# Where the tiles of the second FFN product lie, and in which order its weights are loaded

## The chip, the cores and the metric

The kernel runs on one core of a Trainium2 chip. The metric is the device time of one execution in microseconds (us). The core has TensorE (PE, matmuls), VectorE (DVE), ScalarE (ACT), GpSimd (POOL) and SyncE (SP), whose queue issues the loads from HBM. All five work through instruction streams of their own, in order, and wait on each other by semaphores. SBUF gives each of the 128 partitions some 207 KB to the program's tiles here, which it lays out itself.

## The reference

One step of a decoder layer over 1088 tokens (1024 of a prompt, 8 x 8 of samples) with 1024 channels:

```
x = x + 0.5 * swiglu(rmsnorm(x), w_ffn1_in, w_ffn1_out)
x = x + mixer(rmsnorm(x)) @ w_out        # gated DeltaNet and attention, gated
x = x + 0.5 * swiglu(rmsnorm(x), w_ffn2_in, w_ffn2_out)
y = rmsnorm(x)

swiglu(x, w_in, w_out): gate, up = split(x @ w_in); (silu(gate) * up) @ w_out
```

The hidden width of both FFNs is 2816, 22 blocks of 128. All is float32.

## The kernel before

Each float32 product is made of three matmuls: an operand z is split into hi (ACT casts it, L225) and lo = z - hi (DVE subtracts, L226), and hi·hi, hi·lo and lo·hi are summed in PSUM. So an operand is ready when its load has landed, ACT has cast and DVE has subtracted.

An FFN is two products. `ffn_in` computes the hidden values h from x, in seven Strassen products per pair of 128-blocks, into a gate buffer `sg` (pool of two buffers). `store_h` writes the results to DRAM, `hq` (seven combinations, for 18 blocks) or `hd` (the last four blocks); GpSimd issues these stores. The operands are x7[0] and x7[1], the seven combinations of the two token halves p = 0 (256 columns a matmul) and p = 1 (288). The last pair of blocks runs all seven products of p = 0 first and then all seven of p = 1 (L497), so that x7[0] is done with earlier than x7[1].

`ffn_out` multiplies h by w_out, Strassen again: seven passes j over five groups of blocks (`GROUPS`; four of two block pairs, one of one), and four direct blocks at the end. `rights` loads the h tiles (544 KB) from hq into h0 and h1 in turn and splits them into x0 to x3. `lefts` loads w_out into w0 to w3 and v, one tile per group, in two halves: load(i, 0) brings the rows of a11 and a21 of group i, load(i, 1) those of a12 and a22 (1024 KB each, 512 for group 4). It splits the pass's combination into u0 to u3. GpSimd changes the w tiles in place for later passes (L634, L636), and in pass 2 DVE makes the difference S = a22 - a11 (L629). Nothing of ffn_out can start before x0, u0 of group 0 stand; its matmuls are L689 (hi·hi), L690 (hi·lo of h) and L691.

The order of the instructions on each queue is not that of the code: a scheduler sets it when the program is built, from its own estimate of when places and operands come free; `keep_in_program_order` pins single instructions (the first two splits of each side). What an instruction truly waits for at run time is the last user of the bytes that it writes, and what it reads.

`open_ffn_out` puts the tiles of a second product into one pool growing from the bottom and one ("right") ending at the top, in the order named. The sizes per partition in bytes are acc 34816, tq 26112, w 16384, x 8704, u and v and f 8192, h and r 4352, S 4096. The places are those of the first product's tiles, so a load waits for the last of these. By the sizes the places are, before and after, and what stands there in the last stretch of the first product:

| tile | FFN1 before | FFN1 after | FFN2 before | FFN2 after |
|---|---|---|---|---|
| w0 | sg buffer | x7[0] | x7[1] | x7[0] hi |
| h0, h1 | x7[0] | x7[0] | x7[1] | x7[0] hi |
| w1 | sg buffer | x7[0], "tt" and "xr" | x7[0] lo | x7[0] lo |
| w2 | x7[0] | in tq: x7[1] | x7[0] hi | x7[1] |
| w3 | in tq: x7[1] | sg buffer | x7[0] hi | x7[1], x7[0] hi |
| v | in tq: x7[1] | in tq: x7[1] | "tm" | "tm" |

The last sg buffer is free when the store of hd has landed, x7[0] at the end of p = 0, x7[1] at the end of p = 1. In FFN2 x7[0] is in two parts: its hi lies on the place of an older tile, xhl[0], its lo beside x7[1]. acc lies on x7[1] before and after; x1 and x2 change places, so that x2 instead of x1 overlaps the last sg buffer, as S0 and S1 do.

`ffn_in_first` makes the first pair of blocks of FFN1; its gate tile of token half 1, sg0, takes one of two buffers "raw7" that otherwise hold raw weights (1024 KB loads, `pair_raw`, L297). `turned` transposes x in nine blocks of 128 tokens during ffn_in of FFN1: load into the tile "xr" (L544), TensorE (L551), ACT back into xr (L554), GpSimd's store (L555).

Of the kernel before, what the change touches and what calls it, by code (L numbers as in the profile page):

```python
# [9 lines left out]
F32 = mybir.dt.float32  # L10
# [8 lines left out]
P = 128  # L19
D = 1024  # L20
KD = D // P
# [19 lines left out]
GROUPS = ((0, 2), (2, 2), (4, 2), (6, 2), (8, 1))  # L41
# [69 lines left out]
class Weave:  # L111
# [28 lines left out]
    def run(self, n, *until):  # L140
        self.left += n
        while self.cur is not None or self.left or any(g in until for _, g in self.lat):
            due = [e for e in self.lat if e[0] <= self.t]
            if due:
                e = due[0]
                try:
                    cost, gap = next(e[1])
                    self.t += cost
                    e[0] = self.t + gap
                except StopIteration:  # L150
                    self.lat.remove(e)
            elif not self.fill():
                self.t = min(e[0] for e in self.lat)


class Core:
# [234 lines left out]
    def ffn_in_first(self, st, w_in):  # L391
        nc, v = self.nc, self.nc.vector
# [42 lines left out]
        def quadrants(p, col, h, ts):  # L435
            for k in range(4):
                b = self.tm("b").rearrange("p a b -> p (a b)")[:, :4 * h].rearrange("p (a b) -> p a b", a=4)
                self.xn_chunk(k, [x[t] for t in ts], 2 * h, b)
                oh, ol = (y[:, :, k, col:col + h] for y in self.x7[p])
                self.split(oh[:, 0:4], ol[:, 0:4], b)  # L440
                self.t_parts(b)
                self.split(oh[:, 4:7], ol[:, 4:7], b[:, 1:4])
# [16 lines left out]
        self.columns_t(rows)  # L459
        ug = list(self.units_direct(raws[0]))  # L460
        quadrants(1, 0, P, (4, 5))
        sg = self.rawp.tile([P, KD, 2 * P], F32, tag="raw7", bufs=2, name=self.name("sg0")).rearrange("p a b -> p (a b)")[:, :4 * 288]
        s2 = sg.rearrange("p (m h t) -> p m h t", m=2, h=2)
        direct(1, 0, P, 0, ug, s2)
        norm(*plan[1])
# [12 lines left out]
        sg = self.sg("sg0")  # L478
# [59 lines left out]
    def turned(self):  # L538

        nc = self.nc  # L540
        for t in range(NCH):
            m = min(P, T - t * P)
            xr = self.ttp.tile([P, D], F32, tag="xr", bufs=1, name=self.name("xr"))
            nc.gpsimd.dma_start(xr[:m], self.x_rows(t))  # L544
            for _ in range(4):
                yield
            pts = []
            for hf in range(2):
                pts.append(self.bank("t").rearrange("p (a b) -> p a b", b=P))
                for k in range(4):  # L550
                    nc.tensor.transpose(out=pts[hf][:, k, :m], in_=xr[:m, (4 * hf + k) * P:(4 * hf + k + 1) * P], identity=self.ident[:m, :m])  # L551
            y = xr.rearrange("p (k t) -> p k t", t=P)
            for hf in range(2):
                nc.scalar.copy(y[:, 4 * hf:4 * hf + 4, :m], pts[hf][:, :, :m])  # L554
            nc.gpsimd.dma_start(self.xt[:, :, t * P:t * P + m], y[:, :, :m])  # L555
            for _ in range(5):
                yield

    def open_ffn_out(self, layout):

        shapes = {"acc": [P, 4, 4, HT], "tq": [P, 3, 4, HT], "x": [P, 2, T], "u": [P, 2, D], "h": [P, T], "w": [P, 2, 2, D], "v": [P, 1, 2, D], "S": [P, D], "r": [P, T], "f": [P, 2, D]}
        self.fo = {}
        for stack, side, names in layout:
            pool = self.pool("fo", stack=stack, side=side)
            for nm in names.split():
                k = nm if nm in shapes else nm.rstrip("0123456789")
                self.fo[nm] = pool.tile(shapes[k], F32R if k in "xuf" else F32, name=self.name(nm))
        self.acc = self.fo["acc"]
        if "tq" in self.fo:
            flat = self.fo["tq"].rearrange("p a b c -> p (a b c)")  # L570
            self.fo["w3"] = flat[:, :4 * D].rearrange("p (n k c) -> p n k c", n=2, k=2)
            self.fo["v"] = flat[:, 4 * D:6 * D].rearrange("p (n k c) -> p n k c", n=1, k=2)

    def x(self, k, c):
# [29 lines left out]
    def lefts(self, w_out):  # L604

        fo, dma, g, v = self.fo, self.nc.sync.dma_start, self.nc.gpsimd, self.nc.vector
        ws = [fo[f"w{i}"] for i in range(4)] + [fo["v"]]

        def load(i, k):
            if i < len(GROUPS):  # L610
                p, n = GROUPS[i]
                dma(ws[i][:, :, k], w_out[0, 2 * p * P:2 * (p + n) * P, :].rearrange("(n k p) c -> k p n c", k=2, p=P)[k])

        def quads(i):
            return [ws[i][:, :, k, 512 * h:512 * h + 512] for k in range(2) for h in range(2)]

        at = 0
        for i in range(3):
            load(i, 0)
        for j in range(7):  # L620
            for i in range(len(GROUPS)):
                a11, a21, a12, a22 = quads(i)
                if j == 0:
                    load(i + 3, 0)
                    load(i, 1)
                if j == 2:
                    n = GROUPS[i][1]
                    s = fo[f"S{i % 2}"].rearrange("p (n c) -> p n c", c=512)[:, :n]
                    v.tensor_tensor(out=s, in0=a22, in1=a11, op=ALU.subtract)  # L629
                    g.tensor_tensor(out=a12, in0=a12, in1=s, op=ALU.subtract)  # L630
                out = self.split_to(f"u{at % 4}", (a11, a12, s if j == 2 else None, a11, a22, a21, a12)[j], at < 2)
                at += 1
                if j == 0:
                    g.tensor_tensor(out=a11, in0=a11, in1=a21, op=ALU.subtract)  # L634
                if j == 1:
                    g.tensor_tensor(out=a21, in0=a21, in1=a22, op=ALU.add)  # L636
                yield out
        for i, f in enumerate(DIRECT):
            if i == 0:
                for k in range(2):  # L640
                    dma(fo[f"S{k}"], w_out[0, (f + k) * P:(f + k + 1) * P, :])
            out = self.split_to(f"u{at % 4}", fo[f"S{i % 2}"].rearrange("p (n c) -> p n c", n=1))
            at += 1
            if i < 2:
                dma(fo[f"S{i}"], w_out[0, (f + 2) * P:(f + 3) * P, :])
            yield out
# [986 lines left out]
    def ffn2(self):  # L1633
        nc, v = self.nc, self.nc.vector
        self.lab = ""
        wo = self.i["w_out"].rearrange("o (k p) c -> p (o k) c", p=P)
        with ExitStack() as st:
# [4 lines left out]
            x0 = self.pool("x0", stack=s0).tile([P, KD, 512], F32, name="x0")  # L1642
            x1 = self.pool("x1", stack=s1).tile([P, KD, 576], F32, name="x1")
            ap, aq = self.pool("ain", stack=sa, side="right"), self.pool("ain", stack=sa)
            aq.tile([P, 1408], F32, name="gap")
            a = {h: (aq if h in (4, 5) else ap).tile([P, T], F32, tag="al" if h in (2, 3, 6) else "ah", bufs=2, name=self.name("a")) for h in (2, 3, 0, 1, 4, 5, 6)}
# [101 lines left out]
        order = (0, 2, 1)  # L1748
        with ExitStack() as st:
            self.open_psum(st, t=8)  # L1750
            self.open_ffn_out(((st, None, "u1 u2 u3 x3 x0 u0 S0 S1 x1 x2 v r0 w1"), (st, "right", "h0 h1 w0 acc w2 w3")))
            self.ffn_out(self.i["w_ffn2_out"], self.final(order), self.xd, order, lambda: None)

    def final(self, order):
# [98 lines left out]
    def run(self):  # L1853
        self.setup()
        with ExitStack() as st:
            self.open_psum(st, t=8)
            self.open_ffn_in(st)
            self.table(ACT_FFN)
            self.ffn_in_first(st, self.i["w_ffn1_in"])
            self.ffn_in(self.i["w_ffn1_in"], [(f, up, (0, 1)) for f in range(2, NF, 2) for up in range(2)], self.turned())  # L1860
        order = (0, 2, 1)
        with ExitStack() as st, ExitStack() as se:
            self.open_psum(st, t=8)
            self.open_ffn_out(((st, None, "acc tq x0 u0 x1 u1 x2 u2 x3 u3 S0 f"), (se, "right", "S1 w2 h0 h1 w0 w1")))

            def between():
                se.close()
                self.open_xhl()
                raw = self.fo["S0"].rearrange("p (k c) -> p k c", c=P)
                nc = self.nc  # L1870
                nc.sync.dma_start(raw, self.i["w_in"].rearrange("o (k p) c -> p (o k) c", p=P)[:, :, O_KS:O_KS + P])
                self.first_w = [self.fo["f"][:, i].rearrange("p (k c) -> p k c", c=P) for i in range(2)]
                self.split(*self.first_w, raw)

            self.ffn_out(self.i["w_ffn1_out"], self.to_mixer(order), self.xt, order, between)
        self.mixer()
        self.ffn2()
# [44 lines left out]
```

## Time and profile before

| | us |
|---|---|
| median of 3 runs | 2888.87 (2887.42 to 2890.08) |
| the profiled execution | 2897.63 |
| its span in the profile | 2895.9 |
| TensorE busy | 2703.3 (93%) |

The profile is of one execution; its span is the time from the first to the last instruction, and 1.7 us of the execution's time lie around it. Places in it are given in us from the span's start. FFN1's first product ends at about 544, its second runs from about 578 to beyond 776; FFN2's first product ends at about 2613, its second runs from 2639. A row of a timeline gives the start, the duration, engine, line, operation, the tiles out<-in and, in brackets, how long the engine had been idle before it and what ended this. PE's clock is given as a share of 2.4 GHz; 0.50 is 1.2 GHz.

### The profile page before, as it was taken

How to read it: one execution, taken by the hardware profiler on the slowest of the kernel's cores; microseconds unless marked ns; L12 is line 12 of the kernel's file. 1: busy time of each engine (PE TensorE's matmuls, PEld its weight loads, DVE VectorE, ACT ScalarE, POOL GpSimd, SP SyncE). 2: the span in 40 equal slices, each digit the busy share in tenths (PEclk: the TensorE clock that was granted, in tenths of full speed). 3: DMA queues.
4: the chain of work that ended last, by engine and by line, in shares of the span. 5: the costliest groups of instructions: out<-in, count | busy, mean ns of one | idle time of the engine just before them, and what ended most of it. 6: DMA issues, size and time to landing. Idle time of an engine off the chain costs nothing. (4 is left out here: it accounts for less than half of the span.)

```text
span 2895.9 us, 50870 instructions
## 1 busy us (share of the span) xinstructions
PE 2703.3 (93%) x19839; PEld 2527.8 (87%) x19839; DVE 1987.4 (69%) x4497; ACT 1242.7 (43%) x2919; POOL 656.0 (23%) x625
## 2 busy tenths in 40 slices
PE   6999999599989999999999999999989999996998
PEld 6899999599978888878788888888979999996998
DVE  6677787455563767666786767775689888765545
ACT  5233323133333667663654555556444332322333
POOL 3221221131031211121223121222044122104110
PEclk9999999799999999999999999999999999998999
DMA  3233422454432322344234243324614232216462
GB/s 134 93 127 116 141 99 80 148 160 115 133 103 61 82 64 57 82 106 97 61 92 103 60 100 78 92 65 140 217 62 133 95 113 99 91 53 238 116 151 78
DMA packets 236871, 306.66 MB, mean 106 GB/s; under 512 B 14405, under 2 KB 184214, under 8 KB 236598
## 3 DMA queue, kind: packets, MB, share of 16 engines
q1 hardware_dynamic: 203252, 222.21, 25.5%
q0 software_dynamic: 33312, 81.19, 10.5%
q8 instruction: 156, 2.56, 0.4%
q14 instruction: 85, 0.70, 0.1%
q10 hardware_dynamic: 66, 0.02, 0.0%
HBM read 212.19 MB, written 84.19 MB: 102 GB/s over the span
## 5 line engine op out<-in xcount | busy, mean ns | idle before, releaser
L251 PE MATMUL pst<-x,u 128*128 128x256 f32 (+3 forms) x2640 | 779.3, 295 | 1.0 <-DVE x L226 1.0
L250 PE MATMUL pst<-x,u 128*128 128x256 f32 (+3 forms) x2024 | 609.8, 302 | 18.2 <-ACT x L225 10.5
L252 PE MATMUL pst<-x,u 128*128 128x256 f32 (+3 forms) x2024 | 606.2, 300 | 10.5 <-DVE u L226 10.5
L251 PEld LDWEIGHTS pst<-x,u 128*128 128x128 f32 x2640 | 504.2, 191 | 6.9 <-DVE x L226 1.3
L250 PEld LDWEIGHTS pst<-x,u 128*128 128x128 f32 x2024 | 387.4, 192 | 26.8 <-ACT x L225 12.1
L252 PEld LDWEIGHTS pst<-x,u 128*128 128x128 f32 x2024 | 388.6, 192 | 16.7 <-DVE u L226 12.1
L689 PE MATMUL pst<-x,u 128*128 128x272 f32 x1008 | 290.9, 290 | 50.5 <-ACT x L225 50.5
L225 ACT CAST u<-raw 128x512 fp32r<-128x512 f32 x316 | 190.6, 617 | 304.6 <-PE pst L252 268.8
L252 PE MATMUL psgh<-xhl,wlh 128*128 128x512 f32 (+2 forms) x912 | 304.1, 333 | 0.0
L690 PE MATMUL pst<-x,u 128*128 128x272 f32 x1008 | 292.9, 291 | 5.2 <-DVE x L226 5.2
L691 PE MATMUL pst<-x,u 128*128 128x272 f32 x1008 | 292.4, 290 | 0.0
L226 DVE TENSOR_TENSOR u<-raw,u 128x512 fp32r<-128x512 f32 x316 | 226.6, 725 | 42.6 <-ACT u L225 42.4
L334 DVE TENSOR_TENSOR tm<-pst,tm 128x288 f32<-128x288 f32 (+1 forms) x420 | 177.1, 436 | 104.8 <-PE pst L252 103.2
L252 PE MATMUL pst<-xhl,u 128*128 128x256 f32 (+2 forms) x808 | 235.9, 292 | 3.3 <-DVE u L226 3.3
L250 PE MATMUL pst<-xhl,u 128*128 128x256 f32 (+2 forms) x808 | 236.1, 294 | 2.7 <-ACT u L225 2.7
L689 PEld LDWEIGHTS pst<-x,u 128*128 128x128 f32 x1008 | 190.7, 190 | 51.0 <-ACT x L225 51.0
L690 PEld LDWEIGHTS pst<-x,u 128*128 128x128 f32 x1008 | 191.8, 190 | 5.9 <-DVE x L226 5.9
L691 PEld LDWEIGHTS pst<-x,u 128*128 128x128 f32 x1008 | 191.6, 190 | 0.0
L252 PEld LDWEIGHTS psgh<-xhl,wlh 128*128 128x128 f32 x912 | 173.8, 191 | 12.4
L252 PEld LDWEIGHTS pst<-xhl,u 128*128 128x128 f32 x808 | 152.6, 189 | 7.1 <-DVE u L226 4.1
L250 PEld LDWEIGHTS pst<-xhl,u 128*128 128x128 f32 x808 | 152.2, 189 | 6.0 <-ACT u L225 3.1
L250 PE MATMUL psg<-xhl,whc 128*128 128x512 f32 (+2 forms) x456 | 155.2, 340 | 1.4 <-ACT whc L225 1.4
(693 smaller groups left out, 6454.1 us busy)
## 6 DMA issues: line engine op xcount, KB each, us to landing
raw<-in_w_ffn_in_dram SPq DMA_DIRECT2D x48, 1024.0 KB
h<-hq SPq DMA_DIRECT2D x56, 544.0 KB
hq<-sg POOLq DMA_DIRECT2D x45, 544.0 KB, 3.7
rawh<-in_w_in_dram SPq DMA_DIRECT2D x38, 512.0 KB
w<-in_w_ffn_out_dram SPq DMA_DIRECT2D x14, 1024.0 KB
raw<-in_w_in_dram SPq DMA_DIRECT2D x21, 512.0 KB
ring<-ring SPq DMA_DIRECT2D x32, 272.0 KB
t4h<-tdr POOLq DMA_DIRECT2D x32, 256.0 KB, 5.6
```

The lines of the kernel that those rows point to most:

```text
L225: keep(self.nc.scalar.copy(hi, src))
L226: return keep(self.nc.vector.tensor_tensor(out=lo, in0=src, in1=hi.bitcast(F32), op=ALU.subtract))
L250: nc.tensor.matmul(out, w[0], x[0], start=start, stop=False)
L251: nc.tensor.matmul(out, w[0], x[1], start=False, stop=False)
L252: nc.tensor.matmul(out, w[1], x[0], start=False, stop=stop)
L334: v.tensor_tensor(out=out, in0=pb, in1=t[:, i, :n], op=ALU.add)
L689: nc.tensor.matmul(pb, w[0], y[0], start=first, stop=False, skip_group_check=True)
L690: nc.tensor.matmul(pb, w[0], y[1], start=False, stop=False, skip_group_check=True)
L691: nc.tensor.matmul(pb, w[1], y[0], start=False, stop=end, skip_group_check=True)
```

## The change

The memory maps of both second products, as in the table above; w2 instead of w3 shares the place of tq in FFN1. The order of `load` calls in `lefts`: before, the first halves of groups 0, 1, 2, then in pass 0 at group i load(i+3, 0) and load(i, 1); after, load(0, 0) alone, then (1, 0), (2, 0), (0, 1) at group 1, (3, 0), (1, 1) at group 2, (4, 0), (2, 1) at group 3, (3, 1) at group 4, and (4, 1) at group 0 of pass 1. And sg0 of `ffn_in_first` goes from a raw7 buffer to the tile "xr", which is widened from 1024 to 1152 columns. The pools' sizes stay as they were but for xr. No arithmetic changes.

```diff
--- before.py
+++ after.py
@@ -459,7 +459,7 @@
         self.columns_t(rows)
         ug = list(self.units_direct(raws[0]))
         quadrants(1, 0, P, (4, 5))
-        sg = self.rawp.tile([P, KD, 2 * P], F32, tag="raw7", bufs=2, name=self.name("sg0")).rearrange("p a b -> p (a b)")[:, :4 * 288]
+        sg = self.ttp.tile([P, 4 * 288], F32, tag="xr", bufs=1, name=self.name("sg0"))
         s2 = sg.rearrange("p (m h t) -> p m h t", m=2, h=2)
         direct(1, 0, P, 0, ug, s2)
         norm(*plan[1])
@@ -540,7 +540,7 @@
         nc = self.nc
         for t in range(NCH):
             m = min(P, T - t * P)
-            xr = self.ttp.tile([P, D], F32, tag="xr", bufs=1, name=self.name("xr"))
+            xr = self.ttp.tile([P, 4 * 288], F32, tag="xr", bufs=1, name=self.name("xr"))[:, :D]
             nc.gpsimd.dma_start(xr[:m], self.x_rows(t))
             for _ in range(4):
                 yield
@@ -568,7 +568,7 @@
         self.acc = self.fo["acc"]
         if "tq" in self.fo:
             flat = self.fo["tq"].rearrange("p a b c -> p (a b c)")
-            self.fo["w3"] = flat[:, :4 * D].rearrange("p (n k c) -> p n k c", n=2, k=2)
+            self.fo["w2"] = flat[:, :4 * D].rearrange("p (n k c) -> p n k c", n=2, k=2)
             self.fo["v"] = flat[:, 4 * D:6 * D].rearrange("p (n k c) -> p n k c", n=1, k=2)
 
     def x(self, k, c):
@@ -615,14 +615,17 @@
             return [ws[i][:, :, k, 512 * h:512 * h + 512] for k in range(2) for h in range(2)]
 
         at = 0
-        for i in range(3):
-            load(i, 0)
+        load(0, 0)
         for j in range(7):
             for i in range(len(GROUPS)):
                 a11, a21, a12, a22 = quads(i)
-                if j == 0:
-                    load(i + 3, 0)
-                    load(i, 1)
+                if j == 0 and i:
+                    if i == 1:
+                        load(1, 0)
+                    load(i + 1, 0)
+                    load(i - 1, 1)
+                if j == 1 and i == 0:
+                    load(len(GROUPS) - 1, 1)
                 if j == 2:
                     n = GROUPS[i][1]
                     s = fo[f"S{i % 2}"].rearrange("p (n c) -> p n c", c=512)[:, :n]
@@ -1748,7 +1751,7 @@
         order = (0, 2, 1)
         with ExitStack() as st:
             self.open_psum(st, t=8)
-            self.open_ffn_out(((st, None, "u1 u2 u3 x3 x0 u0 S0 S1 x1 x2 v r0 w1"), (st, "right", "h0 h1 w0 acc w2 w3")))
+            self.open_ffn_out(((st, None, "u1 u2 u3 x3 x0 u0 S0 S1 x2 x1 v r0 w1"), (st, "right", "acc w2 w3 h0 h1 w0")))
             self.ffn_out(self.i["w_ffn2_out"], self.final(order), self.xd, order, lambda: None)
 
     def final(self, order):
@@ -1861,7 +1864,7 @@
         order = (0, 2, 1)
         with ExitStack() as st, ExitStack() as se:
             self.open_psum(st, t=8)
-            self.open_ffn_out(((st, None, "acc tq x0 u0 x1 u1 x2 u2 x3 u3 S0 f"), (se, "right", "S1 w2 h0 h1 w0 w1")))
+            self.open_ffn_out(((st, None, "acc tq S0 x0 u0 x2 u2 x3 u3 f x1 u1"), (se, "right", "h0 h1 w0 w1 w3 S1")))
 
             def between():
                 se.close()
```

## Rows read from the trace of the kernel before

**Rows 1.** The page, part 1: busy us, share and instructions of each engine.

```profile
PE 2703.3 (93%) x19839; PEld 2527.8 (87%) x19839; DVE 1987.4 (69%) x4497; ACT 1242.7 (43%) x2919; POOL 656.0 (23%) x625
```

**Rows 2.** Windows: us, busy us (count) by engine, granted clock, DMA share, GB/s.

```profile
149.00:160.00 11.00, 5.03 (x33) 4.14 (x32) 9.74 (x8) 4.22 (x8) 8.84 (x9) 0.93 0.59 199
160.00:544.00 384.00, 384.00 (x3049) 383.77 (x3049) 291.07 (x515) 118.25 (x243) 72.80 (x70) 0.99 0.30 101
544.00:578.00 34.00, 2.52 (x13) 1.97 (x12) 11.69 (x9) 6.28 (x6) 13.37 (x6) 0.55 0.81 297
560.00:570.00 10.00, 0.00 (x0) 0.00 (x0) 1.47 (x2) 2.09 (x2) 2.34 (x1) 0.50 1.00 398
578.00:776.00 198.00, 198.00 (x1537) 196.73 (x1538) 109.55 (x128) 70.40 (x81) 40.78 (x22) 0.99 0.52 139
2613.00:2640.00 27.00, 2.77 (x13) 2.22 (x12) 11.89 (x8) 6.18 (x6) 11.04 (x5) 0.56 0.89 335
2639.00:2840.00 201.00, 200.73 (x1548) 198.97 (x1549) 113.84 (x130) 71.52 (x81) 44.60 (x23) 0.99 0.53 142
```

**Rows 3.** Timeline of PE: start, us, instruction, count, idle before and releaser.

```profile
577.90 0.60 PE L690 MATMUL pst<-x,u 128*128 128x272 f32 x1 [2.63 <-DVE x L226]
...
2602.18 0.30 PE L250 MATMUL pst<-x,u 128*128 128x288 f32 x1
...
2639.27 0.59 PE L690 MATMUL pst<-x,u 128*128 128x272 f32 x1 [2.58 <-DVE x L226]
```

**Rows 4.** Timeline of the load queue (SPq), 540 to 580.

```profile
544.82 1.35 SPq L612 DMA_DIRECT2D tq<-in_w_ffn_out_dram  x3
557.87 2.15 SPq L612 DMA_DIRECT2D w<-in_w_ffn_out_dram  x4
560.07 1.27 SPq L594 DMA_DIRECT2D h<-hq  x2
```

**Rows 5.** Waits of SP, 540 to 580: us, times, longest.

```profile
SPq L612 <- PE pst L252: 64.5, 1, 64.5
SPq L612 <- DMA hd<-sg: 11.4, 1, 11.4
```

**Rows 6.** Timeline of POOL, 541 to 582.

```profile
546.22 0.72 POOL L519 DMA_DIRECT2D hd<-sg  x1 [41.50 <-DVE sg L341]
...
557.51 2.34 POOL L636 TENSOR_TENSOR tq<-tq 128x1024 f32<-128x1024 f32 x1 [2.10 <-DMA tq<-in_w_ffn_out_dram]
```

**Rows 7.** Timeline of ACT, 544 to 582.

```profile
572.62 1.10 ACT L225 CAST x<-h 128x1088 fp32r<-128x1088 f32 x1 [2.90 <-DMA h<-hq]
```

**Rows 8.** Timeline of DVE, 541 to 582.

```profile
574.40 3.44 DVE L226 TENSOR_TENSOR x<-h,x 128x1088 fp32r<-128x1088 f32 x1
...
578.90 1.28 DVE L226 TENSOR_TENSOR x<-h,x 128x1088 fp32r<-128x1088 f32 x1
```

**Rows 9.** Chain that ended last, 2600 to 2645: start, us, what.

```profile
2613.57 0.37 SPq L612
...
2615.94 16.64 DMA w<-in_w_ffn_out_dram
2632.70 1.36 DVE S L629
...
2635.77 3.46 DVE x L226
```

**Rows 10.** Timeline of DVE, 2600 to 2642.

```profile
2614.07 0.46 DVE L341 TENSOR_TENSOR sg<-sg,tm 128x288 f32<-128x288 f32 x1
2620.34 1.23 DVE L226 TENSOR_TENSOR u<-w,u 128x1024 fp32r<-128x1024 f32 x1 [5.81 <-ACT u L225]
```

**Rows 11.** Waits of SP, 30 to 200: us, times, longest.

```profile
SPq L297 <- DMA hq<-sg: 46.7, 2, 43.5
```

**Rows 12.** Waits of ACT, 100 to 540: us, times, longest.

```profile
ACT xr L554 <- PE pst L551: 18.2, 1, 18.2
```

**Rows 13.** The page, part 6: DMA issues, KB each, us to landing.

```profile
hq<-sg POOLq DMA_DIRECT2D x45, 544.0 KB, 3.7
```

## The prediction

> **What bounds the kernel now.** I read the page first: TensorE is busy in 2703.3 of 2895.9 us, so what a change of layout can bring is in the other 193 us [rows 1]. Then windows on both sides of the two places where a first FFN product gives way to its second product. In 544 to 578 TensorE works 2.52 of 34 us, in 2613 to 2640 it works 2.77 of 27; once the second product runs it has no gap (198.00 of 198, 200.73 of 201) [rows 2]. So two holes, some 33 and 26 us up to the matmuls at 577.90 and 2639.27 from which it runs through [rows 3], hold nearly all that these edits can reach.
>
> What fills the holes is on the load queue (SP). In FFN1 it sits until TensorE's last matmul, issues three loads into the tile tq at 544.82, then sits 11.4 us for the store of hd from sg before it issues w0 at 557.87 and the first h at 560.07 [rows 4, 5]. The store was issued at 546.22 [rows 6]. h0 is behind four w tiles, so its hi cast comes at 572.62 [rows 7]; its lo follows, 3.44 us long and ending at 577.84, and TensorE's full run starts at 577.90 [rows 3, 8]. In FFN2 the chain that ended last reads: loads issued from 2613.57, 16.64 us of a w load, the subtraction S, h0's lo from 2635.77 [rows 9]. No load is issued before the last matmul of the first product, though half p = 0 is done when the 288-column matmuls begin, at 2602.18 [rows 3].
>
> **FFN1.** Before, w0 and w1 lie on the gate buffer sg, w2, h0, h1 on the place of x7[0]. After, h0, h1, w0, w1 lie on x7[0] and the old turning buffer, and w3 and S1 on sg. w0 and h0 so wait for half p = 0 alone. Does SP come to them then? In the rows before, h0's place was free when p = 0 ended, yet h was issued at 560.07 [rows 4]: the instruction order on the queue goes by whole pools of tiles, and the pool "acc tq ..." comes first. w2 and v are in tq now, so I expect three loads into tq at 544.82 again, (2,0), (4,0), (2,1), and w0 and h0 right behind them, without the 11.4 us.
>
> By bytes: those three are 2.62 MB, the store 1.11, w0 1.05, h0 0.56: 5.34 MB. At 398 GB/s, the rate of 560 to 570 [rows 2], that is 13.4 us. The lag on top comes from two rows. The third tq load came in at 557.51 [rows 6]: 12.7 us after issue, less 9.4 us for 3.73 MB, is 3.3. h0's cast at 572.62, 14.75 us after w0's issue, less 11.9 us for 4.75 MB, is 2.85 [rows 4, 7]. So h0 lands at about 544.82 + 13.4 + 3 = 561.2, its hi is done at 562.3 (cast 1.10 [rows 7]), and its lo takes 1.28 us or 3.44 [rows 8]: full run at 563.6 to 565.7. Should w1's first half be ahead of h0, 1.05 MB more, 2.6 us: 568.3. I take 566.5, the middle, a gain of 11.4, called 11. Ends: 14.3 (563.6), and 8 if both w1 and another half tile are ahead.
>
> The DMA page of the Trainium skill ("DMA: Bandwidth & Descriptors", section Specifications) gives about 358 GB/s of HBM for a core; by that 5.34 MB would take 14.9 us and the gain would be 1.5 us less. The row shows 398 in this kernel, with one core running, so the row decides.
>
> **FFN2.** Before, w0, h0, h1 lie on x7[1], which is read up to the last matmul. After, they lie on xhl[0], where p = 0's operands stood: free at 2602.18. w1 stays on the rest of p = 0's operands; acc, w2 and most of w3 lie on x7[1] now. I expect w0 and h0 first on the queue (the pool that holds them is freed as a whole by TensorE, the left one only by the store), issued at 2602.2. 1.61 MB at 398 GB/s is 4 us, with 3 us of lag 2609.3, before p = 1 ends (2613.57 [rows 9]); ACT casts the hi parts at once. DVE has the last combination until 2614.53 [rows 10], then u0's lo (1.23 us [rows 10]) to 2615.8 and h0's lo to 2617.0 or 2619.2, by 1.28 or 3.46 us [rows 8, 9]. Gain against 2639.27: 22.3 or 20.1; I take 21. Bound below: w0 and h0 are issued at 2613.57 after all, but first: with the store 2.72 MB, 6.8 + 3 us, 2623.4, hi and lo 2.4 to 4.6: 2627 at the middle, a gain of 12.
>
> The 1.28 or 3.46 us is where the Trainium skill bears ("SBUF — State Buffer", section Who interferes with whom): a VectorE tensor-tensor on two SBUF inputs and a GpSimd instruction that reads SBUF exclude each other, and the one that starts first runs through. By that rule GpSimd's subtraction (L634), released by u0's lo, loses to h0's lo if that stands ready right behind u0's lo: 1.28, a gain of 22.3, and 3.46 would need a GpSimd instruction already running. The rows have both lengths for the same shape, and I leave the middle.
>
> **What is left over.** The clock is low after either hole (0.55 and 0.56 granted, of 2.4 GHz, in the windows [rows 2]) and stays so for some microseconds, before and after alike: 0. The order of left tiles, S0 and x1 against x2, and "f" behind x3 move tiles whose first use is later than h0's: covered by j = 0, which has six groups of work; bound 2.6 us a product, one half tile at 398 GB/s, if one comes too late. The running second product draws 139 GB/s where 398 were there [rows 2], so starving it beyond that is no case of mine.
>
> **The start.** sg0 leaves a raw7 buffer for the tile "xr". A raw load waited 43.5 us for a store of hq from sg0 [rows 11]; that wait goes, but the load's data was wanted only when the next weights were cast, and from 160 to 544 TensorE has no gap (384.00 of 384 [rows 2]), so 0. In exchange the first turned block loads only when sg0's last store has landed (instead of at the start), and its first transposes come after ffn_in_first anyway. One gap hangs on a turned block already: ACT sits 18.16 us before L554 for the transposes of one block, weight casts queue behind it, and TensorE works 5.03 of 11 us in 149 to 160 [rows 2, 12]: 6 us. If the other order closes it, -6; if the load blocks GpSimd for its wait, +3.7 (a store's landing [rows 13]). I take 0.
>
> **The sum.** -11 - 21 + 0 = -32. The profiled execution took 2897.63 us (span 2895.9), so 2865.6 by its own time; it lies 8.8 above the median 2888.87 of the shown runs, for which the same 32 gives 2857. The main case's own range: FFN1 8 to 14, FFN2 12 to 22, start +4 to -6, stalls up to 5; all ends at once are unlikely, and I take 2846 to 2872.
>
> **Rivals.**
> (a) Both products get early loads: FFN1's w0 and h0 go out when p = 0 ends. In FFN2 half p = 1 takes 11.4 us (2602.18 to 2613.57), so that is near 533.4 here; they land at about 540.4, the lo parts wait only for DVE's last combination, which released the store at 546.22 [rows 6], and full run is at 548.7 to 550.9: FFN1 gains 28, the total is 49, 2840. Against it: the order by pools above [rows 4]. Chance 0.15.
> (b) The S subtraction of the third pass (L629) stays ahead of h0's lo on DVE, as it is in the chain now [rows 9], and now waits for a half tile that is loaded later. Up to (0,1) FFN1 has 7.99 MB, 20.1 us, at 567.9; S 3.2 and lo 3.44 bring 574.5: a gain of 3.4. FFN2, issued behind (2,0) from 2613.57: 3.2 MB, 8.1 + 3 us, 2624.6, S and lo to 2631.2: a gain of 8. Together 11, 2878. DVE's order is set when the program is made, and a half tile that comes later moves S back as well, which speaks against it. Chance 0.1.
> (c) The change doesn't do what it says: SP still comes to w0 and h0 at 557.87, and in FFN2 h0 stays behind the other w tiles. No gain, 2889. Chance 0.07.
> (d) Slower: the turning of x. With sg0 in the tile of xr every turned block shifts against the weight units; the row of 18.16 us shows that one badly placed block costs 6 us [rows 12]. There are nine blocks (the loop of L541). From six more such blocks on it outweighs the 32; with all nine, 8 more than now, 48 - 32 = +16: 2905. For it: ACT's casts are queued behind L554. Against: 160 to 544 runs free of gaps now [rows 2], though blocks are turned there too. Chance 0.07.
>
> **Chances.** Main case 0.61, (a) 0.15, (b) 0.1, (c) 0.07, (d) 0.07. 0.2%, 5.8 us, is about what a measurement here can tell from no change: faster 0.86, same 0.07, slower 0.07. The range goes from (a) to (b), 2838 to 2880, and leaves out (c) and (d).
>
> **What would show it.** SP's issue of w0 and h near 546 instead of 557.87 (FFN1) and near 2602 (FFN2), before the last matmul; no wait for hd ahead of w; the restart at about 566 less the start's shift, and 3.5 to 6 us after the last combination in FFN2; windows of the second products still without a gap; the gap at 149 to 160 where it was. The prediction is wrong if h0 still lands behind several w tiles, if DVE or ACT has another instruction ahead of h0's parts, if half tiles of the first pass come so late that TensorE stops between groups, or if the turning shows new gaps before 544.

## The result, and the profile after

The changed kernel takes 2847.87 us (median of 4 runs, 2846.10 to 2850.15), the kernel before 2888.14 beside it: a ratio of 0.986, with a 95% interval of 0.9843 to 0.9877, 40 us less. The forecast was 32 less, 2857, with 2838 to 2880 as the range. That the two are so near is in part luck, for behind it stand two misses that partly cancel: the start brought some 18 us that I had put at 0, and some 14 us came back in the second products, where I had allowed 2.6 us each and taken none.

The page of the changed kernel, part 1, answers to [rows 1]: TensorE's busy time hardly moves, the span around it does. The changed kernel has three lines more, so the matmuls L689 to L691 are L692 to L694 here, GpSimd's L634 and L636 are L637 and L639, and S (L629) is L632.

```profile
PE 2691.0 (95%) x19839; PEld 2516.7 (88%) x19839; DVE 1997.3 (70%) x4497; ACT 1243.1 (44%) x2919; POOL 659.1 (23%) x625
```

Windows of the changed kernel (columns as in [rows 2]). The gap at 149 to 160 is gone (5.03 of 11 before), the hole in FFN1 goes from 526 to 547.4, and the second products, which had no gap [rows 2], now have some: 193.88 of 196.6 in FFN1, and in FFN2 25.71 of the first 35.6 us behind the first product, the short hole among them.

```profile
149.00:160.00 11.00, 11.00 (x90) 11.00 (x89) 6.05 (x13) 3.04 (x7) 1.63 (x2) 1.00 0.31 100
160.00:526.00 366.00, 366.00 (x2923) 365.63 (x2921) 280.18 (x494) 113.35 (x232) 72.80 (x70) 1.00 0.30 102
526.00:547.40 21.40, 1.60 (x6) 1.18 (x5) 6.74 (x5) 3.76 (x4) 7.75 (x4) 0.58 0.88 325
547.40:744.00 196.60, 193.88 (x1508) 193.69 (x1508) 113.37 (x124) 70.96 (x81) 48.29 (x24) 0.98 0.56 153
2578.40:2614.00 35.60, 25.71 (x196) 24.71 (x195) 33.74 (x17) 10.95 (x12) 25.77 (x10) 0.97 0.84 311
```

The load queue of the changed kernel, around both holes, answers to [rows 4]. In FFN1 the first product ends at 526.1; three loads into tq go out at 526.00, and w0 and the first two h right behind, with no wait for the store of hd. In FFN2 w0 and h0 go out at 2567.27 and 2567.73, 11 us before the first product's last matmul.

```profile
526.00 1.35 SPq L612 DMA_DIRECT2D tq<-in_w_ffn_out_dram  x3
527.40 0.84 SPq L612 DMA_DIRECT2D w<-in_w_ffn_out_dram  x1
528.35 1.19 SPq L594 DMA_DIRECT2D h<-hq  x2
```

```profile
2567.27 0.37 SPq L612 DMA_DIRECT2D w<-in_w_ffn_out_dram  x1
2567.73 0.93 SPq L594 DMA_DIRECT2D h<-hq  x2
2568.72 9.99 SPq L612 DMA_DIRECT2D w<-in_w_ffn_out_dram  x2
```

TensorE's timeline, FFN1 and then FFN2, answers to [rows 3]. Its run begins at 547.46 and at 2581.82, but waits follow, which I call stalls: one in FFN1, 2.66 us for an accumulation by DVE (L669, which takes a finished PSUM tile into acc), and three in FFN2, for a cast, which itself waited for a w load to land, and twice for DVE's lo of a weight unit, 7.4 us together.

```profile
544.04 1.50 PE L692 MATMUL pst<-x,u 128*128 128x272 f32 x5 [17.94 <-ACT x L225]
547.46 0.59 PE L693 MATMUL pst<-x,u 128*128 128x272 f32 x1 [1.92 <-DVE x L226]
...
579.52 0.36 PE L692 MATMUL pst<-x,u 128*128 128x272 f32 x1 [2.66 <-DVE acc L669]
```

```profile
2578.14 0.29 PE L252 MATMUL pst<-x,u 128*128 128x288 f32 x1
...
2581.82 0.40 PE L693 MATMUL pst<-x,u 128*128 128x272 f32 x1 [2.44 <-DVE x L226]
...
2600.65 0.39 PE L692 MATMUL pst<-x,u 128*128 128x272 f32 x1 [1.18 <-ACT u L225]
...
2603.12 0.40 PE L694 MATMUL pst<-x,u 128*128 128x272 f32 x1 [1.95 <-DVE u L226]
...
2613.73 0.59 PE L694 MATMUL pst<-x,u 128*128 128x272 f32 x1 [4.32 <-DVE u L226]
```

The granted clock shifts as well. In FFN1 it is 0.50 (1.2 GHz) from the restart to 553.3, and again from 580.7 to 584.0, just after the stall; in the kernel before it was 0.50 for 3.8 us behind the hole. In FFN2 it stays 1.00 (2.4 GHz) over the short hole and on to 2611.6, then is 0.50 from 2611.7 to 2618.4, from within the last stall on; before it was 0.50 for 4.0 us behind the hole.

DVE and GpSimd in FFN2 just there. h0's lo takes 1.28 us; from 2581.68 on DVE's lo splits take 3.4 us about as often as 1.3, the long ones each behind a GpSimd instruction that had started before them. u<-v, for which TensorE waited last, was cast at 2605.03 (ACT) and came on DVE at 2610.86, behind two such long ones.

```profile
2579.34 1.22 DVE L226 TENSOR_TENSOR u<-w,u 128x1024 fp32r<-128x1024 f32 x1
2580.48 1.28 DVE L226 TENSOR_TENSOR x<-h,x 128x1088 fp32r<-128x1088 f32 x1
2581.68 3.40 DVE L226 TENSOR_TENSOR u<-w,u 128x1024 fp32r<-128x1024 f32 x1
2585.01 1.28 DVE L226 TENSOR_TENSOR x<-h,x 128x1088 fp32r<-128x1088 f32 x1
2586.21 3.41 DVE L226 TENSOR_TENSOR u<-w,u 128x1024 fp32r<-128x1024 f32 x1
...
2604.12 3.42 DVE L226 TENSOR_TENSOR u<-w,u 128x1024 fp32r<-128x1024 f32 x1
2607.46 3.47 DVE L226 TENSOR_TENSOR x<-h,x 128x1088 fp32r<-128x1088 f32 x1
2610.86 2.82 DVE L226 TENSOR_TENSOR u<-v,u 128x512 fp32r<-128x512 f32 x1
```

```profile
2580.70 3.30 POOL L637 TENSOR_TENSOR w<-w 128x1024 f32<-128x1024 f32 x1 [0.26 <-issue]
2585.16 3.38 POOL L637 TENSOR_TENSOR w<-w 128x1024 f32<-128x1024 f32 x1 [1.16 <-DVE u L226]
...
2603.14 3.31 POOL L637 TENSOR_TENSOR w<-w 128x1024 f32<-128x1024 f32 x1 [1.16 <-DVE u L226]
2606.42 3.36 POOL L639 TENSOR_TENSOR w<-w 128x1024 f32<-128x1024 f32 x1
```

The load queue of FFN1's start. The raw load that waited 43.5 us for a store of hq [rows 11] is one of these two, both out by 30.24.

```profile
15.73 14.51 SPq L297 DMA_DIRECT2D raw<-in_w_ffn_in_dram  x2
```

### The profile page after: what moved, and what is told of

It reads as the page before. It is cut to its first block, busy times and chain, and to the rows that moved or that the text cites. A ratio compares the mean times of both kernels' runs of the same rounds, so it can differ in the third digit from the quotient of the medians.

```text
span 2846.9 us, 50867 instructions
## 1 busy us (share of the span) xinstructions
PE 2691.0 (95%) x19839; PEld 2516.7 (88%) x19839; DVE 1997.3 (70%) x4497; ACT 1243.1 (44%) x2919; POOL 659.1 (23%) x625
## 5 line engine op out<-in xcount | busy, mean ns | idle before, releaser
L250 PEld LDWEIGHTS pst<-x,u 128*128 128x128 f32 x2024 | 383.5, 190 | 21.8 <-ACT x L225 12.7
L692 PE MATMUL pst<-x,u 128*128 128x272 f32 x1008 | 291.9, 291 | 21.8 <-ACT x L225 17.9
L694 PE MATMUL pst<-x,u 128*128 128x272 f32 x1008 | 293.8, 292 | 6.3 <-DVE u L226 6.3
L334 DVE TENSOR_TENSOR tm<-pst,tm 128x288 f32<-128x288 f32 (+1 forms) x420 | 176.9, 436 | 101.7 <-PE pst L252 99.9
L692 PEld LDWEIGHTS pst<-x,u 128*128 128x128 f32 x1008 | 191.9, 191 | 22.6 <-ACT x L225 18.2
L694 PEld LDWEIGHTS pst<-x,u 128*128 128x128 f32 x1008 | 192.7, 191 | 6.7 <-DVE u L226 6.7
L252 PEld LDWEIGHTS psgh<-xhl,wlh 128*128 128x128 f32 x912 | 173.2, 190 | 12.2
```

What stands on the lines that cost most here:

```text
L250: nc.tensor.matmul(out, w[0], x[0], start=start, stop=False)
L252: nc.tensor.matmul(out, w[1], x[0], start=False, stop=stop)
L334: v.tensor_tensor(out=out, in0=pb, in1=t[:, i, :n], op=ALU.add)
L692: nc.tensor.matmul(pb, w[0], y[0], start=first, stop=False, skip_group_check=True)
L694: nc.tensor.matmul(pb, w[1], y[0], start=False, stop=end, skip_group_check=True)
```

## The experiments

The table reads each profile in the same way. "First product" is the start of its last matmul in FFN1. A hole goes from the end of the last matmul of a first product to the matmul from which TensorE runs on, short waits after it apart; "passes" from there to the start of the last matmul of the seven passes, stalls included. All in us; the time is the median, that of the kernel before beside it in brackets.

| kernel | time | first product | hole, FFN1 | passes, FFN1 | hole, FFN2 | passes, FFN2 |
|---|---|---|---|---|---|---|
| before | 2888.1 | 544.6 | 33.0 | 191.1 | 25.7 | 191.2 |
| changed | 2847.9 (2888.1) | 525.8 | 21.4 | 196.4 | 3.4 | 199.6 |
| gate tile only | 2868.5 (2886.3) | 527.5 | 33.5 | 191.3 | 25.7 | 191.6 |
| maps and order only | 2868.0 (2886.3) | 541.0 | 21.2 | 196.4 | 3.4 | 199.1 |
| changed, old order | 2862.4 (2886.3) | 525.5 | 30.1 | 191.3 | 22.9 | 190.9 |
| FFN2 only | 2873.2 (2886.3) | 541.6 | 32.8 | 190.9 | 3.4 | 200.0 |
| new order only | 2883.2 (2887.7) | 544.4 | 24.5 | 199.2 | 8.9 | 203.7 |
| without GpSimd's operations | 2834.8 (2886.9) | 528.2 | 18.1 | 192.6 | 3.4 | 191.0 |
| GpSimd later | 2849.3 (2886.9) | 526.7 | 21.8 | 196.4 | 3.4 | 200.0 |
| h from ACT's queue | 2856.1 (2886.9) | 528.0 | 18.4 | 199.7 | 3.4 | 206.6 |
| pool cut in two | 2833.4 (2886.9) | 527.8 | 3.4 | 199.7 | 3.4 | 199.1 |
| in place on DVE | 2837.1 (2888.7) | 527.5 | 17.8 | 193.2 | 4.6 | 194.8 |
| pool cut, in place on DVE | 2831.3 (2888.7) | 527.9 | 4.6 | 198.8 | 4.6 | 194.7 |
| turned block later | 2888.3 (2888.7) | 541.2 | 32.8 | 192.0 | 25.6 | 191.7 |

From the end of FFN1's passes to the end of FFN2's first product the work is the same in all of them; it took 1827.6 to 1844.3 us in these profiles, the longest in the profile of before. That is most of why the two profiled executions differ by 49 us (2897.63 and 2848.63) and the medians by 40. The column of the first product varies too: 541.0 to 544.6 in the five profiles with the old gate tile, 525.5 to 528.2 in the nine with the new one.

**The parts.** First, the gate tile alone in the kernel before.

```diff
-        sg = self.rawp.tile([P, KD, 2 * P], F32, tag="raw7", bufs=2, ...)
+        sg = self.ttp.tile([P, 4 * 288], F32, tag="xr", bufs=1, name=self.name("sg0"))
...
-            xr = self.ttp.tile([P, D], F32, tag="xr", ...)
+            xr = self.ttp.tile([P, 4 * 288], F32, tag="xr", ...)[:, :D]
```

> Kernel before with only the gate tile sg0 moved into the tile xr. My theory now: this edit alone makes the start shorter, because the raw weight load that waited 43.5 us for the store goes out by about 30 us, and because the turned block no longer holds ACT at 149: the first FFN1 product ends about 18.8 us earlier (near 526), nothing else changes, about 2869 us. Rival, the prediction's own step (the raw load is wanted late, the start gains 0, and what was gained there came with the new maps): the product still ends near 544, 2885 to 2889 us.

2868.45 us, ratio 0.9938 (0.9922 to 0.9955), 17.9 us less; the first product ends at 527.8 and TensorE has no gap at 149 (11.00 of 11 us). So this edit alone makes the start shorter, and the step "the start: 0" of the prediction falls. Whether by the reasons that the expectation gives is another question; see the last experiment.

Second, the changed kernel with that edit undone.

```diff
-        sg = self.ttp.tile([P, 4 * 288], F32, tag="xr", bufs=1, name=self.name("sg0"))
+        sg = self.rawp.tile([P, KD, 2 * P], F32, tag="raw7", bufs=2, ...)
```

> Changed kernel with the gate tile sg0 put back into a raw7 buffer: only maps and load order are new. My theory: the first FFN1 product ends near 544 again, both holes stay short (21 us in FFN1, 3.4 in FFN2) and some 13 us are given back behind them, together about -21: 2867 us. Rival (the start's gain belongs to the maps): near 2848 us.

2868.04 us, again 0.9938 (0.9922 to 0.9955): 18.3 us less by maps and order. Both holes are as short as in the changed kernel. The gap at 149 is there again, and so is ACT's wait of 18.2 us for the transposes:

```profile
149.00:160.00 11.00, 6.68 (x36) 6.23 (x36) 10.53 (x11) 4.40 (x9) 5.91 (x6) 0.78 0.62 217
```

Third, FFN2 alone: its map, and the load order there only.

```diff
-  "u1 u2 u3 x3 x0 u0 S0 S1 x1 x2 v r0 w1"), (st, "right", "h0 h1 w0 acc w2 w3")
+  "u1 u2 u3 x3 x0 u0 S0 S1 x2 x1 v r0 w1"), (st, "right", "acc w2 w3 h0 h1 w0")
...
+        new = "tq" not in fo
+        for i in range(1 if new else 3):
...
```

> Kernel before with map and load order of FFN2's second product alone. My theory: the hole goes from 25.7 to about 3.4 us (-22.3) and 7 to 8.5 us come back as stalls between the groups of the first pass: 2873 to 2875 us. Rival (the stalls come from something else that changed, FFN2 keeps the whole): 2866 us.

2873.15 us, ratio 0.9955 (0.9940 to 0.9970), 13.2 us less. The hole falls by 22.3 and the passes grow by 8.8, as in the changed kernel. Gate tile 17.9, FFN2 13.2, and 5.1 for FFN1 (18.3 less 13.2) make 36.2 of the 40.3; the intervals of the parts, some 5 us to either side, are wide enough for the rest.

Fourth and fifth, the load order undone in the changed kernel, and the new order alone in the kernel before (the same edit the other way round).

```diff
-        load(0, 0)
+        for i in range(3):
+            load(i, 0)
...
-                if j == 0 and i:
...
+                if j == 0:
+                    load(i + 3, 0)
+                    load(i, 1)
```

> Changed kernel with the load order of before (first halves of groups 0, 1, 2 first). Theory that map and order are both needed: w2's first half, whose place is freed only by the end of the first product, stands ahead of h0 on the queue in FFN2, so the hole there grows from 3.4 to some 10 to 13 us, and in FFN1 h0 comes 3 to 5 us later; some of the later stalls go as the tiles are there earlier: 2853 to 2862 us. Rival (the scheduler sorts the loads by the places, so the order in the code means nothing): within 3 us of 2848.

> Kernel before with the new load order alone, maps and sg0 as before. By the prediction's sums: in FFN1 h0 follows w0 directly after the wait for the store, so the hole falls from 33 to 22 to 24 us; in FFN2 w0 and h0 are issued at the end of the first product, but first, so the hole falls from 25.7 to about 13 us; some 4 us and 6 to 8 us come back as stalls in the first pass: 2876 to 2881 us. Rival (the order is worth something only where the maps let w0 go early): 2886 to 2889 us.

With the old order 2862.42 us, ratio 0.9918 (0.9898 to 0.9939), 16.4 us more than the changed kernel, by what each is under the kernel before beside it (23.9 and 40.3), and just above what was expected. But the holes grew by 8.7 and 19.5 us, where the expectation had 3 to 5 and some 7 to 10, and the passes gave back 5.1 and 8.7: so the total came near by misses that cancel. Its load queue in FFN2 goes early too, at 2563.94, but h stands behind five w loads, of which one waits for the end of the first product, until 2577.44; the hole is 22.9 us.

```profile
2563.94 13.40 SPq L612 DMA_DIRECT2D w<-in_w_ffn_out_dram  x5
2577.44 1.15 SPq L594 DMA_DIRECT2D h<-hq  x2
```

The order alone brought 4.5 us, ratio 0.9986 (0.9976 to 0.9995), less than the 7 to 12 expected. The holes shrank by 8.5 and 16.8 us, more than expected in FFN2, and the passes grew by 8.1 and 12.5: 0.4 and 4.3 us are left. The wait shifts into the passes, where TensorE waits for DVE as in the changed kernel (4.7 us for L669 in FFN1, 7.7 us for lo parts in FFN2). The order alone is worth 4.5 us, the maps with the old order 6.0 (23.9 less the 17.9 of the gate tile), both together 18.3: map and order need each other.

**Where 14 us came back.** The passes of the changed kernel are 5.3 us longer in FFN1 and 8.4 in FFN2; 2.7 and 7.4 of that are stalls, the rest is the clock at 0.50. Two theories on the stalls: H, DVE is the engine without slack in the first pass and GpSimd's in-place operations hold it up; Q, w loads stand behind h loads that wait for DVE. First, GpSimd's two operations are left out (L637 and L639 of the changed kernel; j goes from 0 to 6, so what stands under j == 7 never runs).

```diff
-                if j == 0:
-                    g.tensor_tensor(out=a11, in0=a11, in1=a21, op=ALU.subtract)
-                if j == 1:
+                if j == 7:
                     g.tensor_tensor(out=a21, in0=a21, in1=a22, op=ALU.add)
```

> Changed kernel without GpSimd's two in-place operations on the weight tiles in passes 0 and 1 (a11 - a21 and a21 + a22 are left out, so the later passes multiply other numbers; loads, splits and matmuls are all there). Theory H (the 7.4 us of stalls and the slow clock behind the restart of FFN2 come because DVE's two-input operations take 3.4 us instead of 1.25 while GpSimd works on SBUF, and DVE is the engine with no slack there): DVE's rows return to about 1.25 us, stalls in FFN2 fall from 7.4 to 2 or less, in FFN1 from 2.7 to 0, 2836 to 2841 us. Theory Q (w loads wait behind h loads on SP's queue, so tiles come late): the stalls stay at 5 us or more, 2845 to 2849 us.

2834.79 us, ratio 0.9814 (0.9797 to 0.9830). TensorE has no stall behind either hole, the passes are at 192.6 and 191.0 again, and DVE's first rows at 1.22 to 1.28 us, where the same four took 1.22, 1.28, 3.40 and 1.28 above:

```profile
2573.96 1.22 DVE L226 TENSOR_TENSOR u<-w,u 128x1024 fp32r<-128x1024 f32 x1
2575.10 1.28 DVE L226 TENSOR_TENSOR x<-h,x 128x1088 fp32r<-128x1088 f32 x1
2576.30 1.22 DVE L226 TENSOR_TENSOR u<-w,u 128x1024 fp32r<-128x1024 f32 x1
2577.43 1.28 DVE L226 TENSOR_TENSOR x<-h,x 128x1088 fp32r<-128x1088 f32 x1
```

That is H, and a little more than expected of it, since the hole in FFN1 is 3.3 us shorter as well. Q is not wholly out by this: an h load waits for DVE's lo, so a quick DVE also frees the queue.

Next, GpSimd's first operation moved to the next pass in the code.

```diff
-                if j == 0:
+                if j == 1:
                     g.tensor_tensor(out=a11, in0=a11, in1=a21, op=ALU.subtract)
-                if j == 1:
                     g.tensor_tensor(out=a21, in0=a21, in1=a22, op=ALU.add)
```

> Changed kernel with GpSimd's a11 - a21 of pass 0 made one pass later, in front of a21 + a22; everything is computed. Theory H: GpSimd is quiet while the first pass starts, 4 to 6 of the 7.4 us of stalls in FFN2 go and the 2.7 us in FFN1, unless the operations only bunch up in pass 1: 2840 to 2845 us. Theory Q: no difference, 2846 to 2850 us.

2849.33 us, no difference; but it tells nothing on H or Q, since the scheduler put the operation where it was: GpSimd's first one stands right behind the store, as it did at 2580.70 above:

```profile
2576.42 0.72 POOL L519 DMA_DIRECT2D hd<-sg  x1 [41.33 <-DVE sg L341]
2577.40 3.28 POOL L637 TENSOR_TENSOR w<-w 128x1024 f32<-128x1024 f32 x1 [0.27 <-issue]
```

Then the h loads from ACT's queue.

```diff
-        fo, dma = self.fo, self.nc.sync.dma_start
+        fo, dma = self.fo, self.nc.scalar.dma_start
```

> Changed kernel with all h loads issued from ACT's queue instead of SP's, so that no w load stands behind an h load that waits for DVE. Theory Q: the w loads of groups 2 and 3 go out 3 to 5 us earlier in FFN2 and the stalls fall below 3 us, 2840 to 2844 us. Theory H: the wait for a w load (1.2 us) goes, the waits for DVE's lo parts (1.95 and 4.3 us) stay, and ACT's casts now stand behind h's waits, 2845 to 2855 us.

2856.12 us, ratio 0.9894 (0.9879 to 0.9909), slower than the changed kernel and a microsecond over what H expected. The w loads do go out earlier (that into v at 2585.29 instead of 2598.46) and the time grew all the same, which speaks against Q but doesn't rule it out. For the passes of FFN2 grow to 206.6 by a new wait: now ACT's own casts and copies stand behind h, and TensorE waits 7.0 us for one of ACT's.

```profile
PE pst L692 <- ACT acc L667: 7.0, 1, 7.0
```

Then, GpSimd's two operations given to DVE.

```diff
-                    g.tensor_tensor(out=a11, in0=a11, in1=a21, op=ALU.subtract)
+                    v.tensor_tensor(out=a11, in0=a11, in1=a21, op=ALU.subtract)
...
-                    g.tensor_tensor(out=a21, in0=a21, in1=a22, op=ALU.add)
+                    v.tensor_tensor(out=a21, in0=a21, in1=a22, op=ALU.add)
```

> Changed kernel with the two in-place operations of passes 0 and 1 (a11 - a21, a21 + a22) on DVE instead of GpSimd; everything is computed. Theory H: DVE pays about 1.2 us for each of its own instead of up to 2.2 us for each operation that GpSimd blocks, so the stalls in FFN2 fall from 7.4 to 1 to 4 us and in FFN1 from 2.7 to 0 to 1: 2838 to 2844 us. Rival (DVE has no slack at all in the first pass, its own ten short operations cost what the blocking cost): 2846 to 2852 us.

2837.11 us, ratio 0.9827 (0.9809 to 0.9845) against 0.986 (0.9843 to 0.9877) of the changed kernel, a microsecond under H's range; the two intervals only just touch. DVE does more of its own and TensorE waits less: FFN1 has no stall, FFN2 one of 2.4 us for DVE, the passes are 193.2 and 194.8, and the hole in FFN2 grows by the 1.2 us of one such operation ahead of h0's lo. With the same loads and the same operations on another engine the stalls fall by two thirds or more, as in the run without them, so it is GpSimd's work beside DVE's that made most of them.


```profile
2578.91 1.22 DVE L226 TENSOR_TENSOR u<-w,u 128x1024 fp32r<-128x1024 f32 x1
2580.16 1.23 DVE L637 TENSOR_TENSOR w<-w 128x1024 f32<-128x1024 f32 x1
2581.30 1.28 DVE L226 TENSOR_TENSOR x<-h,x 128x1088 fp32r<-128x1088 f32 x1
```

**Why FFN1 kept a hole of 21 us.** The prediction said that the queue's order goes by whole pools. Here w3 and S1, the two tiles on the gate buffer, get a pool of their own on the same bytes.

```diff
-  (se, "right", "h0 h1 w0 w1 w3 S1")
+  (se, "right", "w3 S1"), (se, "right", "h0 h1 w0 w1")
```

> Changed kernel with FFN1's right pool cut in two: w3 and S1, which lie on the gate buffer, in a pool of their own on the same bytes, h0, h1, w0, w1 in another. Theory P (the order on the load queue goes by when whole pools come free, so in FFN1 w0 and h0 stand behind the three loads into tq because w3 and S1 in their pool wait for the store): w0 and h0 are issued when half p = 0 ends, near 515 instead of 527.4, the hole in FFN1 shrinks from 21.4 to 3.4 to 6 us, up to 5 us more come back as stalls as they do in FFN2: 2832 to 2838 us. Rival (what sets the order is not the pool): 2846 to 2850 us.

2833.35 us, ratio 0.9814 (0.9799 to 0.9830). w0 goes out at 516.89, before the first product's end, and the loads into tq come behind it; the hole falls to 3.4 us, the passes grow by 3.3 more.

```profile
516.89 0.37 SPq L612 DMA_DIRECT2D w<-in_w_ffn_out_dram  x1
517.36 0.92 SPq L594 DMA_DIRECT2D h<-hq  x2
...
527.95 0.37 SPq L612 DMA_DIRECT2D tq<-in_w_ffn_out_dram  x1
```

So rival (a) was open to this layout: two tiles that wait for a store, in the same pool, cost 18 us of hole. The last kernel has this pool and the in-place operations on DVE.

> The kernel with FFN1's pool cut in two, and the in-place operations on DVE as well. If both theories hold they add: 3 to 9 us under the 2833 of the cut pool, 2824 to 2830 us. Rival as for the kernel with DVE alone: 2833 to 2838 us.

2831.29 us, ratio 0.9802 (0.9785 to 0.9820): the lowest here, some 57 us under the kernel before, but not clear of the cut pool alone, and between the two expectations. FFN2's passes gain 4.4 us and FFN1's only 0.9, and each hole grows by 1.2. So with the early restart what the two theories promised adds up in FFN2 but hardly in FFN1: there TensorE still stalls 5.6 us for DVE's accumulation (L669), with GpSimd's two operations gone.

**What closed the gap at 149.** In the kernel before, with the old gate tile, every turned block comes one product later.

```diff
             nc.gpsimd.dma_start(self.xt[:, :, t * P:t * P + m], y[:, :, :m])
-            for _ in range(5):
+            for _ in range(6):
                 yield
```

> Kernel before with each turned block of x one product later (six steps instead of five between two blocks); sg0 stays in raw7. Theory T (the gap at 149 is the turned block's: ACT's copy L554 stands ahead of seven weight casts and waits for the transposes): the copy stands behind the casts now, the gap and its slow clock go, the first product ends 8 to 10 us earlier, 2877 to 2880 us. Theory W (the gap is the late raw load's, whatever stands on ACT): no change, 2885 to 2889 us.

2888.25 us, ratio 1.0005 (0.9994 to 1.0016): nothing, so theory T is out. ACT casts the weights at 129.97 now and no longer waits for the transposes, but DVE makes their lo at 148.62 only, behind the combinations of the running products (L334, L341), and ACT's next cast waits for DVE. So the gap isn't the turned block's; but it isn't a late load's either, as theory W has it, for the data was there to be cast at 129.97, 19 us before DVE came to it.

```profile
129.97 0.62 ACT L225 CAST u<-raw 128x512 fp32r<-128x512 f32 x1
153.40 0.62 ACT L225 CAST u<-s 128x512 fp32r<-128x512 f32 x1 [22.81 <-DVE s L311]
```

```profile
148.24 0.46 DVE L341 TENSOR_TENSOR sg<-sg,tm 128x288 f32<-128x288 f32 x1
148.62 0.68 DVE L226 TENSOR_TENSOR u<-raw,u 128x512 fp32r<-128x512 f32 x1
```

The trace of the kernel before says the same of both places where its start loses time. The waiting raw load went out at 79.24 and the next at 113.06. From 90 to 100 and from 120 to 124 nothing is on its way (2 and 0 GB/s), so both had landed; ACT is idle 9.47 us and yet casts the weights at 100.76, behind a cast of x, and those of the other place at 150.25.

```profile
90.00:100.00 10.00, 10.00 (x44) 8.08 (x43) 3.37 (x4) 0.53 (x2) 0.00 (x0) 1.00 0.01 2
120.00:124.00 4.00, 4.00 (x35) 4.00 (x35) 2.66 (x7) 2.65 (x6) 0.87 (x1) 1.00 0.00 0
```

```profile
99.81 1.05 ACT L225 CAST x<-t 128x1024 fp32r<-128x1024 f32 x1 [9.47 <-PE pst L252]
100.76 0.61 ACT L225 CAST u<-raw 128x512 fp32r<-128x512 f32 x1
...
150.25 0.63 ACT L225 CAST u<-raw 128x512 fp32r<-128x512 f32 x1
```

## Why the prediction was right, and where it was not

**The hole in FFN1** was right in mechanism and size: a gain of 11.4 from the sums, "called 11", and 11.6 measured (33.0 to 21.4). tq first, w0 and h right behind it, no wait for hd; h0's cast came at 542.89, 16.9 us after the first load, where the sum had 16.4, and its lo took 3.38 us. The 566.5 was no true middle: that of 563.6 and 568.3 is 566.0, a gain of 11.9, and the sum's own case with a lo of 3.44 us gives 12.2. The measured 11.6 lies near all of them.

**The hole in FFN2** was right: 20.1 to 22.3, taken 21, and 22.3 measured, the early issue at the end of p = 0 included. The two ends were h0's lo at 3.46 or 1.28 us, and it took 1.28. The rule of the Trainium skill ("SBUF — State Buffer", section Who interferes with whom) gave that end: h0's lo started at 2580.48 and GpSimd's L637 at 2580.70, behind it, so DVE held. In FFN1 GpSimd started first, at 543.90, and DVE's 544.02 took 3.38. The trace agrees with the rule in both.

**"The start: I take 0"** failed, not in its premise but in what I drew from it. That the raw load's "data was wanted only when the next weights were cast" held at run time, as the last experiment shows. From that I took the load's wait for all that the edit could change. It also changed the order of the work on the engines: DVE makes the first combination (L309) of the first three pairs of weights at 89.64, 101.17 and 119.80 in the changed kernel, at 103.60, 113.92 and 151.76 before. The profile after and the gate tile alone show 18.8 and 17.1 us at the end of the first product. Read against the kernel before, TensorE is 4.0 us ahead by its 360th matmul, 9.3 by the 400th and 18.5 by the 760th: two places, at 100 and at 150, where weights were short. I took the second for the turned block's, since ACT's row of 18.16 us stood there [rows 12]; the later turned block shows that it only stood in the same place. Why the scheduler ordered the work otherwise, by its estimate of the load's wait or by something else in the edit, no run here separates.

**"Starving it beyond that is no case of mine"** failed: I counted bytes, 139 GB/s drawn against 398, and bounded the give-back by 2.6 us a product. It was 5.3 in FFN1 and 8.4 in FFN2. Bytes were not the limit of the stalls, 2.7 and 7.4 us of it: without GpSimd's two operations they are 0 with the same loads. When the wait for the loads goes, DVE is late next: in FFN2 it is busy 33.74 of 35.6 us behind the first product, stretched by GpSimd. Where the holes stayed long (30.1 and 22.9 us with the old order) the same DVE work is done in time, and the passes have no stall. The rest of the give-back, 2.6 and 1.0 us, is the clock, which the prediction put at 0, "before and after alike": it was at 0.50 for 9 us instead of 3.8 in FFN1 and for 6.7 instead of 4.0 in FFN2, and in FFN2 the stalls, not the hole, came before its fall. So two of the signs that I named failed, the second products "still without a gap" and "the gap at 149 to 160 where it was".

**The rivals.** (a), early loads in FFN1 too, did not happen, for the reason given, the order by pools, which the cut pool shows. (b) did not: S comes behind h0's lo in both FFNs. (c) did not: the queue's rows show the early issue. (d) did not: there is no gap from 160 to 526, and moving the turned blocks made no difference.

The sum of the profile's terms is -18.8 (start) - 6.3 (FFN1, 11.6 less 5.3) - 13.9 (FFN2, 22.3 less 8.4) = -39.0, against -40.3 of the medians. Mine was 0 - 11 - 21. The first term is the least sure: between the means of the profiles with the old gate tile and with the new one lie 15.4 us, between the medians of the gate tile alone and of the kernel before 17.9.

## What to carry to other kernels

A hole that loads leave is also the time in which other engines get ahead; before costing its closing at its full length, add up what each engine has to do in the first stretch behind it, with the durations that it has while the others run. Where a scheduler sets the order, an edit to one tile's place can move other work on every engine, so look for it in each queue, and not only at the wait that the edit removes. And where a scheduler takes pools as one, give tiles with the same releaser a pool of their own: here w0 then went out at 516.89 instead of 527.40.

## What the runs showed of the hardware that was not expected

The size of GpSimd's share in DVE's time: the same DVE split of 128 x 1024 took 1.22 us alone and 3.4 us behind a GpSimd operation that had started before it (2581.68 behind 2580.70), and GpSimd's own took 2.36 us when it started first (543.90) and 3.30 when DVE had (2580.70). So moving the two in-place operations to DVE, for 1.2 us each, made the kernel faster than having them done beside it (2837.1 against 2847.9).
